# Diagonal blocks of sixteen recurrence steps computed beside the last gate tiles, and a second inverse on GpSimd there

## The chip, the cores and the metric

One core of one Trainium2 chip runs the whole kernel. The metric is the device time of one execution in microseconds (us); three timed runs of the kernel before have a median of 1893.08.

## The reference, cut to what matters

Two trunk layers over 1024 latent tokens behind 256 context tokens, 1024 channels wide. The first layer has bidirectional RWKV-7 time mixing with 12 heads of 64; the change lies in its recurrence. For each head and direction a 64 x 64 state is carried over 1280 tokens:

```python
def rwkv7_scan(r, w, k, v, kk, bb, s0, reverse):
    def step(s, inp):
        r_t, w_t, k_t, v_t, kk_t, b_t = inp
        sa = jnp.einsum('bhij,bhj->bhi', s, kk_t)
        s = s * w_t[:, :, None, :] - sa[..., None] * b_t[:, :, None, :] + v_t[..., None] * k_t[:, :, None, :]
        return s, jnp.einsum('bhij,bhj->bhi', s, r_t)
```

The output of the scan is normed, multiplied by a SiLU gate, and projected; the second layer (retention) follows and isn't touched.

## The kernel before

**Stages.** `phaseA` makes the input projection of layer one in tiles of 128 features: for each of six pairs of heads the keys, values and receptances, then the operands of the recurrence, which go to DRAM (`AR`, `BK`, `VT`). Its last four products are gate tiles (`gate_blocks`, L576), which need nothing but TensorE, a tanh on ScalarE and one product on VectorE for each of three blocks of tokens, so that their time can be shared. `phaseB` is the recurrence; `phaseCD` is everything after it.

**The recurrence in chunks.** 64 tokens make a chunk. A step handles one chunk of four (direction, pair) slots of two heads each, and 20 steps run through the 1280 tokens; three groups of pairs make NS = 60 steps in one row. Inside a chunk the sequential recurrence becomes a triangular system. For step s, `scores(s)` (L1117) multiplies the operands BK[s] and AR[s] into two PSUM tiles PSC (32 matmuls), and `masked(s)` (L1125, VectorE) writes them to the tile SC[s] with the triangle's mask. The system's 64 x 64 triangle is inverted in two halves: the two 32 x 32 diagonal blocks by substitution, row after row, and the block below them by two products (`offd1`, `offd2`) in the step before.

**The inverse of the diagonal blocks.** Eight steps make a group m, so group 0 is steps 0 to 7. `diag(s)` (L1134) stores the diagonal blocks of two steps from SC to a DRAM tile DN; `gather(s)` (L1147) loads four steps' blocks into TL, one block on each of 128 partitions; `inv(m)` (L1176) runs 31 rows, each a multiplication (L1185, tp<-zz,tl) and an addition (L1187, zz<-zz,tp), both with two SBUF operands, on VectorE for group 0 and on GpSimd for all others. Then it stores the inverse (DZ) and its turned copy (DX) on GpSimd's queue, and `bring(q)` (L1199) loads them for the four steps of q into SC and into the tile ZS (two and four loads on SP's queue). Step s can't do its `offd1(s + 1)` before bring of (s + 1) // 4.

**Order.** The order on each engine and queue is that in which the program issues; nothing is reordered. `phaseB` is a generator that the gate tiles call: once ahead of them, and then behind each of the nine pieces of a tile (four pieces of the first four k, then the rest of the three blocks in one, two and two). The first three calls load, the next eight (from behind the third piece of tile 1 to behind the first of tile 2) make scores, masks and stores of steps 0 to 7, and each call after them issues one or two rows of group 0's inverse. `rows(n)` (L1288) counts the calls (st.tick), issues a due gather or bring, and then n rows.

**Between the gates and step 0.** When the gates are done, buffers are opened on their memory; SP loads BK of five more steps into spare buffers (bky), ScalarE's queue the AR; eight steps (PR) are scored ahead, of which EA = 3 have had AR loaded during the gates; their diagonal blocks are stored from ScalarE's queue; bring(0) and bring(1) follow bky on SP's queue. Then `offd1(0)` and `offd2(0)`, and step 0.

**A step.** WT1 = scores x values (L1440, wu), its copy on ScalarE (L1441), offd1 of the next step, product with the inverse (L1454), scores of a step ahead, state (L1473 to L1479), output (L1486, L1494), offd2 and the turned operands (`tok`, L1173, from the loads br) of the next step. At the steps in CU = (2, 5, 8) one further step is scored at the end (`more`, L1391), until the scores are L = 19 steps ahead. GpSimd's rows are issued in the four slots of a step.

Of the kernel before, what the change touches and what calls it, by code (L numbers as in the profile page):

```python
# [41 lines left out]
NR = 2  # L42
CU = (2, 5, 8)
PR = 8
EZ = 1
ER = (2,1,2)
SW = 5
GB = 4
EA = 3
LL = 19  # L50
# [972 lines left out]
def phaseB(g):  # L1023
# [35 lines left out]
    def slots(pool, n0, n1, a0, a1, z):  # L1059
        for i in range(a0, a1):  # L1060
            ARR.append(pool.tile([128, 4, 128], F32, name=f"arr{i}"))
        for i in range(n0, n1, 2):
            SCP.append(pool.tile([128, 2, 4, 2, 128], F32, name=f"scr{i}"))
            SCR.extend(SCP[-1][:, j] for j in range(2))
        for i in z:
            ZS.append(pool.tile([128, 4, 4, 64], F32, name=f"zs{i}"))
            nc.gpsimd.memset(ZS[i], 0.0)

# [8 lines left out]
    TLS = [ip.tile([128, 32, 32], F32, name=f"tl{i}") for i in range(NTL)]  # L1077
    ZZT = ip.tile([128, 32, 32], F32, name="zz")
    TPT = ip.tile([128, 256], F32, name="tp")
    BR, AR, BK, VU, SC, BT, Y, PCS, DN = {}, {}, {}, {}, {}, {}, {}, {}, {}  # L1080
    st = Ctx()
# [12 lines left out]
    def load_v(k):  # L1094

        if k < NS // 2:
            VU[k] = st.rp.tile([128, 2, 4, 2, 64], F32, tag="vu", name=f"vu{k}", bufs=2)
            if k % 10 == 0:
                nc.gpsimd.memset(VU[k][0:64, 0], 0.0)
            (nc.scalar if VQ else nc.sync).dma_start(VU[k][64:128].rearrange("p c x h v -> p c x (h v)"), g.D["VT"][k // 10][:, 2 * k % 20 : 2 * k % 20 + 2])  # L1100
# [33 lines left out]
    def diag(s):  # L1134

        if s % 2 == 0:
            return
        m, c = divmod(s - 1, 8)
        if c == 0:
            DN[m] = dr.tile([2, 8 * steps(m), 32, 32], F32, tag="dn", name=f"dn{m}")  # L1140
        for b in range(2):
            bs = slice(32 * b, 32 * b + 32)
            st.q.dma_start(DN[m][b, 8 * c : 8 * c + 16].rearrange("u s t -> s u t"), pair_of(s)[bs, :, :, :, bs].rearrange("s c x h t -> s (c x h) t"))
        if c % 4 == 2:
            dgs.append((s, st.tick + TD))

    def gather(s):  # L1147
# [28 lines left out]
    def inv(m):  # L1176

        U, eng = 16 * steps(m), nc.gpsimd if m else nc.vector
        TL, ZZ, tp = TLS[m % NTL][:U], ZZT[:U], TPT[:U]
        eng.memset(ZZ, 0.0)  # L1180
# [141 lines left out]
    for s in range(E):  # L1322
# [872 lines left out]
```

## Time and profile before

| | us |
|---|---|
| median of three timed runs | 1893.08 |
| lowest, highest | 1881.7, 1895.54 |
| the profiled execution | 1888.2 |
| its span, first to last instruction | 1886.4 |

The profile is of one execution. Its page gives busy times by engine; the other views (table by stage, chain of waits, order of time of one engine, groups by line, DMA issues) are cuts of the same trace, in us from the span's start. PE is TensorE, DVE VectorE, ACT ScalarE, POOL GpSimd, SPq and ACTq the queues from which SP and ScalarE issue DMAs. L1187 is line 1187 of the kernel before. A matmul's duration overlaps the next one's, so sixteen in a row take less than their sum. "Idle before" in brackets names what released the instruction.

### The profile page before, as it was taken

What the parts mean: (1) busy time and instruction counts of PE and PEld (TensorE: products, weight loads), DVE (VectorE), ACT (ScalarE), POOL (GpSimd) and SP (SyncE); (2) the same over time, 40 slices, a digit from 0 to 9 for tenths busy, and PEclk for the clock granted to TensorE, in tenths of its full rate; (3) what the DMA queues carried; (4) which work ended last, traced back from release to release, by engine and by line L of the source; (5) the groups of instructions that cost most, each with busy time, mean ns of one, the idle gap of its engine ahead of it and who ended that gap; (6) DMA issues with size and microseconds to landing.
All of it is one profiled execution on the core that took longest, in us unless ns stands there. A gap on an engine that the chain in (4) does not pass through costs nothing.

```text
span 1886.4 us, 39626 instructions
## 1 busy us (share of the span) xinstructions
PE 1712.2 (91%) x16450; PEld 1453.3 (77%) x16450; DVE 968.8 (51%) x1524; ACT 697.1 (37%) x1538; POOL 748.3 (40%) x837
## 2 busy tenths in 40 slices
PE   6999998979888876988887878999999999999898
PEld 4777776767666776887776767889898898898786
DVE  6542589888985743444542335453443433524543
ACT  5322454635431143564564544442221311212321
POOL 4331344444442157677778311123333414414300
PEclk9999999989998987898997788999999999999999
DMA  9571265546559486677777744342111101101163
GB/s 321 173 240 59 79 180 141 158 127 187 137 155 281 142 219 166 182 205 201 206 181 164 174 145 143 134 134 83 36 46 45 45 23 57 56 23 56 51 206 100
DMA packets 326727, 257.66 MB, mean 137 GB/s; under 512 B 93756, under 2 KB 276532, under 8 KB 326292
## 3 DMA queue, kind: packets, MB, share of 16 engines
q1 hardware_dynamic: 306468, 218.16, 41.0%
q10 hardware_dynamic: 15456, 20.45, 3.7%
q0 software_dynamic: 4624, 16.52, 2.5%
q8 instruction: 130, 2.13, 0.5%
q14 instruction: 49, 0.40, 0.1%
HBM read 177.16 MB, written 77.91 MB: 135 GB/s over the span
## 4 chain that ended last, share of the span: by engine, by line
PE 44%; DMA 8%; POOL 6%; issue 5%; DVE 4%; ACT 2%; SPq 0%; ACTq 0%; POOLq 0%; DVEq 0%
PE pv L1849 6%; PE pg L1793 5%; PE pq L1793 5%; PE pk L1793 5%; PE pow_oo L1588 4%; PE pow_eo L1588 3%; POOL zz L1187 2%; POOL tp L1185 2%; PE pst L1939 2%; DMA vu<-scr_VT 2%; DMA br<-scr_BK 2%; PE psc L1123 2%; PE wu L1440 1%; PE pkc L1793 1%; PE pgb L586 1%
## 5 line engine op out<-in xcount | busy, mean ns | idle before, releaser
L531 PE MATMUL pgm<-hh,wh 128*128 128x512 f32 (+1 forms) x624 | 170.3, 382 | 0.0
L509 POOL TENSOR_TENSOR wl<-wr,wh 128x512 fp32r<-128x512 f32 x60 | 86.1, 1439 | 190.6 <-ACT wh L507 176.6
L531 PE MATMUL pgm<-hl,wh 128*128 128x512 f32 (+1 forms) x624 | 160.4, 366 | 0.4 <-POOL hl L467 0.4
L531 PE MATMUL pgm<-hh,wl 128*128 128x512 f32 (+1 forms) x624 | 160.1, 365 | 0.0
L1185 POOL TENSOR_TENSOR tp<-zz,tl 128x60 f32<-128x60 f32 (+23 forms) x217 | 110.7, 510 | 65.8 <-DMA tl<-dn 50.0
L1187 POOL TENSOR_TENSOR zz<-zz,tp 128x60 f32<-128x60 f32 (+23 forms) x217 | 118.5, 546 | 17.0
L531 PEld LDWEIGHTS pgm<-hl,wh 128*128 128x128 f32 x624 | 106.8, 195 | 21.0 <-POOL hl L467 1.5
L531 PEld LDWEIGHTS pgm<-hh,wl 128*128 128x128 f32 x624 | 106.5, 194 | 19.2
L531 PEld LDWEIGHTS pgm<-hh,wh 128*128 128x128 f32 x624 | 104.0, 197 | 20.9 <-issue 6.2
L1476 DVE TENSOR_TENSOR inc<-inc,state 128x256 f32<-128x256 f32 x54 | 23.4, 433 | 185.0 <-ACT scr L1165 73.8
L1849 PE MATMUL pv<-wv,hh 128*128 128x256 f32 x640 | 117.2, 285 | 0.0
L554 DVE SCALAR_TENSOR_TENSOR m<-pgm,dv,m 128x255 f32<-128x255 f32 (+2 forms) x108 | 105.1, 987 | 11.2 <-ACT m L544 8.4
L1849 PEld LDWEIGHTS pv<-wv,hh 128*128 128x128 f32 x640 | 99.6, 192 | 0.1
L1588 PE MATMUL pow_eo<-w_eo,yhw_eo 128*128 128x512 f32 x320 | 90.6, 405 | 0.0
L1849 PE MATMUL pv<-wv,hl 128*128 128x256 f32 x320 | 90.5, 283 | 0.0
L1129 DVE TENSOR_TENSOR scr<-psc,mask 128x512 f32<-128x512 f32 x112 | 71.7, 682 | 17.4 <-PE psc L1123 17.4
L1123 PE MATMUL psc<-arr,bkp 64*64 64x128 f32 x1728 | 71.0, 294 | 9.2 <-DVE scr L1129 3.9
L1588 PE MATMUL pow_oo<-w_oo,yhw_oo 128*128 128x512 f32 x256 | 73.3, 403 | 0.0
L1588 PEld LDWEIGHTS pow_eo<-w_eo,yhw_eo 128*128 128x128 f32 x320 | 61.3, 193 | 15.1 <-issue 0.3
L1793 PE MATMUL pg<-hh,wg 128*128 128x512 f32 x256 | 72.2, 393 | 0.0
L818 POOL TENSOR_TENSOR ar<-m,Pp 128x640 f32<-128x640 f32 (+2 forms) x30 | 36.5, 1226 | 87.0 <-ACT Pp L810 82.8
L1793 PE MATMUL pq<-hh,wq 128*128 128x512 f32 x256 | 70.1, 391 | 0.0
(347 smaller groups left out, 4227.6 us busy)
## 6 DMA issues: line engine op xcount, KB each, us to landing
aw<-ada_w SPq DMA_DIRECT2D x16, 1024.0 KB, 9.6
wr<-w_ev SPq DMA_DIRECT2D x60, 256.0 KB, 3.9
scr_AR<-ar SPq DMA_DIRECT2D x24, 640.0 KB, 3.7
scr_BK<-bk SPq DMA_DIRECT2D x24, 640.0 KB, 4.5
br<-scr_BK ACTq DMA_DIRECT2D x60, 256.0 KB, 3.8
arr<-scr_AR SPq DMA_DIRECT2D x55, 256.0 KB, 4.0
bkp<-scr_BK SPq DMA_DIRECT2D x55, 256.0 KB, 5.2
x<-xin SPq DMA_DIRECT2D x20, 512.0 KB, 4.1
```

The lines of the kernel that those rows point to most:

```text
L509: nc.gpsimd.tensor_tensor(out=wl, in0=wr, in1=wh.bitcast(F32), op=ALU.subtract)
L531: g.nc.tensor.matmul(ps[:, b, :n], lhsT=st[:, k % 4, :], rhs=mv[:, k, c0 : c0 + n], start=(k == 0 and i == 0), stop=(k == 7 and i == 2))
L554: nc.vector.scalar_tensor_tensor(out=o, in0=i, scalar=g.muc[:, q, ft : ft + 1], in1=o, op0=ALU.mult, op1=ALU.add)
L818: nc.gpsimd.tensor_tensor(out=ar[:, cs, 64:128], in0=ch(proc(self.r, d, lo, n)), in1=Pp[:, cs, 1:65], op=ALU.mult)
L1123: mm(ps[h][H[m], 128 * x : 128 * x + 128], lhsT=BK[s][H[h], x, H[m]], rhs=AR[s][H[h], x, :], start=True, stop=True, tile_position=(64 * h, ...
L1129: tt(out=out, in0=p.rearrange("p (d q t) -> p d q t", d=2, q=2), in1=K["mask2"].unsqueeze(2).broadcast_to([128, 2, 2, 128]), op=ALU.mult)
L1185: eng.tensor_tensor(out=tv, in0=ZZ[:, 0:k, s : s + 1].broadcast_to([U, k, n]), in1=TL[:, s : s + 1, s + 1 : 32].broadcast_to([U, k, n]), o ...
L1187: eng.tensor_tensor(out=zo, in0=zo, in1=tv, op=ALU.add)
L1588: self.g.nc.tensor.matmul(ps[:, 512 * b : 512 * b + 512], lhsT=st[:, k, :], rhs=mv[:, 512 * b : 512 * b + 512], start=(k == 0 and i == 0), ...
L1793: mm(ps[:, 512 * b : 512 * b + n], lhsT=st[:, k, :], rhs=mv[:, k, o : o + n], start=(k == 0 and i == 0), stop=(k == 7 and i == 2))
L1849: mm(ps[:, 256 * e : 256 * e + 256], lhsT=st[:, k, c0 : c0 + 128], rhs=mv[:, k, :], start=(k == 0 and i == 0), stop=(k == 7 and i == 2))
L1939: mm(ps[:, 128 * (i - i0) : 128 * (i - i0) + 128], lhsT=o.kz[d][:, t], rhs=o.v[:, t], start=True, stop=True)
```

## The change

During the second gate tile, behind scores(7), eight new calls `blocks(s)` (s = 8, 10, ... 22) compute only the square scores from which the diagonal blocks of steps 8 to 23 come: each loads the first 64 columns of AR and BK of two steps (two loads on SP's queue, 256 KB each in pieces of 256 B, two steps ahead of use except the first two), multiplies them (16 matmuls of 64 x 64 by 64 columns), copies the four diagonal parts on ScalarE and stores them from ScalarE's queue. No mask is applied. Groups 1 and 2 gather from there, and `diag` does nothing for these steps. Group 1's inverse is issued two rows a call from then on, beside group 0's, with temporaries of its own; group 0 must be issued to its end before the gates' memory is given up. Group 0's results are stored from SP's queue instead of GpSimd's. bring(0) is issued ahead of the loads for the scores, and bring(2) at its own time. No AR is loaded ahead for steps 8 to 10 (EA = 0), four steps are scored before step 0 instead of eight (PR), and seven steps score one more (CU). The zero fills of ZS, VU and Y2P move from GpSimd to VectorE.

```diff
-CU = (2, 5, 8)
-PR = 8
+CU = (1, 2, 3, 4, 5, 7, 9)
+PR = 4
+EB = 24
+EP = 2
-EA = 3
+EA = 0
@@ slots (and the same in load_v, and for Y2P)
-            nc.gpsimd.memset(ZS[i], 0.0)
+            nc.vector.memset(ZS[i], 0.0)
@@
-    ZZT = ip.tile([128, 32, 32], F32, name="zz")
-    TPT = ip.tile([128, 256], F32, name="tp")
+    ee = ExitStack()
+    ex = ee.enter_context(tc.tile_pool(name="exB", bufs=1, reuse_waits="tile"))
+    ZZT = [p.tile([128, 32, 32], F32, name=f"zz{i}") for i, p in enumerate((ex, ip))]
+    TPT = [p.tile([128, 256], F32, name=f"tp{i}") for i, p in enumerate((ex, ip))]
@@ diag
-        if s % 2 == 0:
+        if s % 2 == 0 or E <= s < EB:
             return
...
+    def blocks_load(s):
+
+        if s < EB:
+            DA[s], DB[s] = (ex.tile([128, 2, 4, 64], F32, tag=t, name=f"{t}{s}", bufs=2) for t in ("dka", "dkb"))
+            for o, n in ((DA, "AR"), (DB, "BK")):
+                nc.sync.dma_start(o[s], g.D[n][s // 20][:, s % 20 : s % 20 + 2, :, 0:64])
+
+    def blocks(s):
+
+        spread(s)
+        c = s % 8
+        for j in range(2):
+            for x in range(4):
+                for h in range(2):
+                    mm(PSC[h][0:64, 256 * j + 64 * x : 256 * j + 64 * x + 64], lhsT=DB[s][H[h], j, x], rhs=DA[s][H[h], j, x], start=True, stop=True, tile_position=(64 * h, 0))
+        dg = ex.tile([64, 2, 4, 2, 32], F32, tag="dg", name=f"dg{s}", bufs=2)
+        for b in range(2):
+            bs = slice(32 * b, 32 * b + 32)
+            for h in range(2):
+                nc.scalar.copy(dg[bs, :, :, h].rearrange("p c x t -> p (c x) t"), PSC[h][bs].rearrange("p (a t) -> p a t", t=64)[:, :, bs])
+            nc.scalar.dma_start(DN[s // 8][b, 8 * c : 8 * c + 16].rearrange("u s t -> s u t"), dg[bs].rearrange("s c x h t -> s (c x h) t"))
+        if c % 4 == 2:
+            dgs.append((s + 1, st.tick + TD))
+        blocks_load(s + 4)
@@ inv
-        TL, ZZ, tp = TLS[m % NTL][:U], ZZT[:U], TPT[:U]
+        TL, ZZ, tp = TLS[m % NTL][:U], ZZT[m > 0][:U], TPT[m > 0][:U]
+        out = nc.gpsimd if m else nc.sync
...
-        nc.gpsimd.dma_start(DZ, ZZ)
+        out.dma_start(DZ, ZZ)
...
-        nc.gpsimd.dma_start(DX, TL[: U // 2])
+        out.dma_start(DX, TL[: U // 2])
@@ rows
-        if back and st.tick >= back[0][1] and (back[0][0] == 0 or len(ZS) == 3 and back[0][0] != 2 and st.s >= 4 * back[0][0] - 3 - back[0][0] % 2):
+        if back and st.tick >= back[0][1] and (back[0][0] == 0 or len(ZS) == 3 and st.s >= 4 * back[0][0] - 3 - back[0][0] % 2):
@@ behind the scores of steps 0 to 7
+    def both():
+
+        n = ER[st.tick % len(ER)]
+        if ivs and ivs[0][0] == 0:
+            for _ in range(EP):
+                if len(ivs) > 1 and st.tick >= ivs[1][2]:
+                    row(1)
+            rows(n)
+        else:
+            rows(EP)
+
+    blocks_load(E)
+    blocks_load(E + 2)
+    for s in range(E, EB, 2):
+        blocks(s)
+        both()
+        yield
     while not g.a_done:
-        rows(ER[st.tick % len(ER)])
+        both()
         yield
+    while ivs and ivs[0][0] == 0:
+        row()
+    ee.close()
@@ before step 0
     st.q = nc.scalar
+    while back and back[0][0] == 0:
+        bring(*back.pop(0))
     load_v(0)
...
-    while back:
+    while back and back[0][0] < 2:
         bring(*back.pop(0))
```

## Rows read from the trace of the kernel before

**Rows 1.** The page of the profile: its span.

```profile
span 1886.4 us, 39626 instructions
```

**Rows 2.** The table by stage (core 0): a stretch in us, its length, busy us of each engine with its instructions, granted TensorE clock, busy share of the DMA engines, GB/s.

```profile
616.41:630.88 14.47, 14.12 (x73) 11.75 (x72) 13.61 (x31) 2.82 (x5) 2.58 (x2) 1.00 0.19 63
647.20:666.90 19.70, 12.48 (x293) 10.67 (x285) 10.44 (x17) 2.60 (x8) 3.95 (x7) 0.83 0.95 239
718.90:731.00 12.10, 0.25 (x6) 0.26 (x6) 0.78 (x2) 0.37 (x1) 4.79 (x10) 0.62 0.80 237
```

**Rows 3.** The chain of work that ended last, followed back from 735 us: start us, us, what.

```profile
720.58 7.17 DMA dx<-tl
727.76 2.71 DMA scr<-dx
...
730.75 0.95 PE inc L1219 x13
```

**Rows 4.** ScalarE in order of time, one line (L1441, one copy in each step; in the order shown those of steps 4, 5, 6, 7 and 15): start us, us, engine, line, operation, out<-in, shape, count, and in brackets the idle time before it and its releaser.

```profile
705.20 0.37 ACT L1441 COPY wt<-wu 128x256 f32<-128x256 f32 x1
...
713.61 0.37 ACT L1441 COPY wt<-wu 128x256 f32<-128x256 f32 x1 [2.81 <-PE wu L1440]
...
718.92 0.37 ACT L1441 COPY wt<-wu 128x256 f32<-128x256 f32 x1 [0.21 <-PE wu L1440]
...
738.30 0.37 ACT L1441 COPY wt<-wu 128x256 f32<-128x256 f32 x1 [0.22 <-PE wu L1440]
...
797.17 0.37 ACT L1441 COPY wt<-wu 128x256 f32<-128x256 f32 x1 [1.20 <-PE wu L1440]
```

**Rows 5.** TensorE in order of time, same columns: the product for step 16's off-diagonal block, in step 15.

```profile
793.31 0.98 PE L1235 MATMUL py<-zs,y2p 128*64 128x32 f32 x16 [1.94 <-DMA zs<-dz]
```

**Rows 6.** TensorE in order of time, the second of the last four gate tiles: first product behind the tile's second piece, behind its third, and the next tile's first.

```profile
606.03 0.28 PE L586 MATMUL pgb<-hh,wh 128*128 128x256 f32 x1
...
607.77 0.28 PE L586 MATMUL pgb<-hh,wh 128*128 128x256 f32 x1
...
616.41 0.28 PE L586 MATMUL pgb<-hh,wh 128*128 128x256 f32 x1
```

**Rows 7.** SP's queue (issue of step 7's diagonal blocks), and VectorE's mask of step 7 ahead of it.

```profile
607.67 0.86 SPq L1143 DMA_DIRECT2D dn<-scr  x2
...
604.28 1.29 DVE L1129 TENSOR_TENSOR scr<-psc,mask 128x512 f32<-128x512 f32 x2 [1.50 <-PE psc L1123]
```

**Rows 8.** DMA issues of the whole execution: out<-in, engine, operation, count, KB each, median us from issue to landing.

```profile
arr<-scr_AR SPq DMA_DIRECT2D x55, 256.0 KB, 4.0
bkp<-scr_BK SPq DMA_DIRECT2D x55, 256.0 KB, 5.2
```

**Rows 9.** DMA queues from 655.4 to 665.7 us, when nearly all packets were of 128 B (9567 of 9968 under 512 B): packets, MB, share of 16 engines' time.

```profile
q1 hardware_dynamic: 5576, 1.19, 54.6%
```

**Rows 10.** TensorE in order of time: sixteen matmuls with 64 columns in step 1.

```profile
680.87 0.69 PE L1486 MATMUL pyo<-scr,vu 128*64 128x64 f32 x16
```

**Rows 11.** VectorE, then GpSimd, in order of time where both read SBUF: in the last products of the operands (566 to 572), and in group 0's inverse (621.6).

```profile
566.97 0.80 DVE L820 SCALAR_TENSOR_TENSOR bk<-th,kk 128x640 f32<-128x640 f32 x1
567.99 2.07 DVE L821 TENSOR_TENSOR ar<-kk,Pp 128x640 f32<-128x640 f32 x1 [0.23 <-issue]
569.98 1.88 DVE L822 SCALAR_TENSOR_TENSOR bk<-bk,Pi 128x640 f32<-128x640 f32 x1
...
621.62 1.52 DVE L1187 TENSOR_TENSOR zz<-zz,tp 128x207 f32<-128x207 f32 x1
...
567.98 1.39 POOL L818 TENSOR_TENSOR ar<-m,Pp 128x640 f32<-128x640 f32 x1 [4.52 <-ACT Pp L810]
569.36 1.81 POOL L509 TENSOR_TENSOR wl<-wr,wh 128x512 fp32r<-128x512 f32 x1
...
621.61 1.29 POOL L509 TENSOR_TENSOR wl<-wr,wh 128x512 fp32r<-128x512 f32 x1 [10.10 <-ACT wh L507]
```

**Rows 12.** VectorE's groups of instructions by line from 620.42 to 643.0 us (rows 8 to 31 of group 0's inverse): count, busy us, mean ns, idle us before.

```profile
L1187 DVE TENSOR_TENSOR zz<-zz,tp 128x192 f32<-128x192 f32 (+15 forms) x24 | 9.9, 411 | 0.8
L1185 DVE TENSOR_TENSOR tp<-zz,tl 128x192 f32<-128x192 f32 (+15 forms) x24 | 9.7, 403 | 0.7
```

**Rows 13.** GpSimd's groups of instructions by line from 680.3 to 710.8 us (rows 1 to 24 of group 1's inverse), same columns.

```profile
L1187 POOL TENSOR_TENSOR zz<-zz,tp 128x192 f32<-128x192 f32 (+15 forms) x24 | 13.8, 576 | 1.9
L1185 POOL TENSOR_TENSOR tp<-zz,tl 128x192 f32<-128x192 f32 (+15 forms) x24 | 12.9, 538 | 30.9 <-DMA tl<-dn 29.1
```

**Rows 14.** Between the gates and step 0: VectorE's turned copy of group 0, SP's queue, and TensorE in order of time.

```profile
643.01 1.13 DVE L1192 COPY tl<-zz 64x1024 f32<-64x1024 f32 x1
...
639.08 15.13 SPq L1092 DMA_DIRECT2D bky<-scr_BK  x5
...
664.70 1.07 PE L1235 MATMUL py<-zs,y2p 128*64 128x32 f32 x16 [2.60 <-DMA zs<-dz]
666.90 1.34 PE L1440 MATMUL wu<-vu,scr 128*64 128x64 f32 x15 [1.13 <-ACT scr L1165]
```

**Rows 15.** TensorE in order of time: the transposes at the end of step 1, and the extra scores at the end of step 5.

```profile
683.03 0.63 PE L1173 MATMUL pt<-ident,br 128*128 128x128 f32 x4 [1.03 <-DMA br<-scr_BK]
...
711.21 0.43 PE L1123 MATMUL psc<-arr,bkp 64*64 64x128 f32 x4 [1.03 <-DVE scr L1129]
711.81 1.09 PE L1123 MATMUL psc<-arr,bkp 64*64 64x128 f32 x28 [0.16 <-DVE scr L1129]
```

More of the change, by code (lines that the diff above doesn't have):

```diff
@@ L1077, in phaseB @@
     TLS = [ip.tile([128, 32, 32], F32, name=f"tl{i}") for i in range(NTL)]
-    ZZT = ip.tile([128, 32, 32], F32, name="zz")
-    TPT = ip.tile([128, 256], F32, name="tp")
-    BR, AR, BK, VU, SC, BT, Y, PCS, DN = {}, {}, {}, {}, {}, {}, {}, {}, {}
+    ee = ExitStack()
+    ex = ee.enter_context(tc.tile_pool(name="exB", bufs=1, reuse_waits="tile"))
+    ZZT = [p.tile([128, 32, 32], F32, name=f"zz{i}") for i, p in enumerate((ex, ip))]
+    TPT = [p.tile([128, 256], F32, name=f"tp{i}") for i, p in enumerate((ex, ip))]
+    BR, AR, BK, VU, SC, BT, Y, PCS, DN, DA, DB = {}, {}, {}, {}, {}, {}, {}, {}, {}, {}, {}
     st = Ctx()
@@ L1098, in load_v @@
             if k % 10 == 0:
-                nc.gpsimd.memset(VU[k][0:64, 0], 0.0)
+                nc.vector.memset(VU[k][0:64, 0], 0.0)
             (nc.scalar if VQ else nc.sync).dma_start(VU[k][64:128].rearrange("p c x h v -> p c x (h v)"), g.D["VT"][k // 10][:, 2 * k % 20 : 2 * k % 20 + 2])
@@ L1134, in diag @@
     def diag(s):
-        if s % 2 == 0:
+        if s % 2 == 0 or E <= s < EB:
             return
         m, c = divmod(s - 1, 8)
-        if c == 0:
-            DN[m] = dr.tile([2, 8 * steps(m), 32, 32], F32, tag="dn", name=f"dn{m}")
+        spread(s - 1)
         for b in range(2):
@@ L1145, in diag, with spread @@
             dgs.append((s, st.tick + TD))
+    def spread(s):
+        if s % 8 == 0:
+            DN[s // 8] = dr.tile([2, 8 * steps(s // 8), 32, 32], F32, tag="dn", name=f"dn{s // 8}")
+    def blocks_load(s):
[19 more added lines that the diff above has]
+        blocks_load(s + 4)
     def gather(s):
@@ L1282, in phaseB, with row @@
     st.tick, st.wait, st.s = 0, SW, -1
-    def row():
-        if next(ivs[0][1], 0) == 0:
-            ivs.pop(0)
+    def row(i=0):
+        if next(ivs[i][1], 0) == 0:
+            ivs.pop(i)
     def rows(n):
@@ L1341, in phaseB @@
         Y2P.append(cq.tile([128, 2, 4, 64], F32, name=f"y2p{i}"))
-        nc.gpsimd.memset(Y2P[i], 0.0)
+        nc.vector.memset(Y2P[i], 0.0)
     tail.gen = tail.eg.enter_context(tc.tile_pool(name="gen", bufs=2, space=PSUM, reuse_waits="tile"))
```

## The prediction

> **What bounds the kernel now.** Start with the page and the table by stage. The profiled execution took 1888.2 us, 1.8 of them outside its 1886.4 us span [rows 1]; the sum below is made against it. The three timed runs have a median of 1893.08 and lie 13.8 us apart, so the sum may stand some 5 us under what is measured. All that changes lies between 577 and 800 us, and the table by stage [rows 2] shows that each stretch there has another limit. In the third of the last four gate tiles (616.4 to 630.9) TensorE is full, 14.12 of 14.47 us, and VectorE nearly so; between the gates and step 0 (647.2 to 666.9) TensorE is filled for 12.48 of 19.70; from 718.9 to 731.0 it stands: 0.25 us of work in 12.10.
>
> That stand is the target, and the chain of waits names its cause [rows 3]. Step 7 needs the corner blocks of steps 8 to 11. Their inverse (group 1) and its turned copy keep GpSimd until the store at 720.58, which takes 7.17 us; a load of 2.71 us follows, and TensorE goes on at 730.75. On ScalarE each step shows by one copy (L1441): 5.31 us for step 6, a plain one, 8.41 for step 5, which scores one step more, and 19.38 for step 7 [rows 4]. The stand so costs 19.38 - 5.31 = 14.1 us; the granted clock falls to 0.62 in that stretch.
>
> **Gain 1: group 1 is ready before step 7.** Its inverse is now made during the gates. By the working below it ends some 6 us after group 0's, at about 674, and is stored by 690; step 7 comes near 740. So -14.1. Nothing is next in its place there: group 2, also early, is wanted at step 15, where TensorE now waits 1.94 us for its zs [rows 5]: -1.9.
>
> **Cost 1: the second gate tile.** phaseB gets one call behind each of the nine pieces of a tile, and scores(7) stands after the first piece of tile 2, so the eight `blocks` calls stand after its other eight, the first at 606.0 [rows 6]. Its own loads are issued only there, in program order on SP's queue behind group 0's diagonal store (L1143), which waits for VectorE's mask of step 7 and went out at 607.67 [rows 7]. With six loads fewer in front I put it at 606.5 (between 605.6, the end of that mask, and 607.7). The pair of loads then goes out at 607.4 and 607.85. A load of 256 KB lands in 4.0 us (5.2 for bkp) [rows 8]; those come in rows of 2 KB, the new ones in pieces of 256 B. 128 B pieces took 54.6% of 16 engines for 10.3 us for 5576 packets, 16 ns each [rows 9], so 1024 of them keep 16 engines busy for about 1.0 us: no new bound, and I take 4.0. First wait: 607.85 + 4.0 + 0.2 - 606.0 = 6.0 us (4 to 9), with all later gate matmuls queued behind it. Each call's 16 matmuls of 64 columns cost 0.7 (16 such took 0.69, L1486 [rows 10]; bounds 0.5 and 1.0): 8 x 0.7 = 5.6. Loads for s+4 go out when blocks(s) has read its buffer: 0.65 + 4.0 + 0.15 = 4.8 us to landing, while TensorE has one piece, one call and one piece between, 4.2 at first (1.74 each, 606.03 to 607.77), then 3.5 (1.4 each, the rest to 616.41). Counting each wait as cover for the next pair leaves 0.6, 0.4, 0.9, 0.4, 0.9, 0.4 = 3.6 (0 to 9). ScalarE's four copies (0.37 each, as L1441 for as many elements a lane [rows 4]) and two issues (0.43 each, half of L1143's pair [rows 7]) per call, 2.3, fit beside this; without that cover each call would wait some 0.2. Tile 2 grows by 6.0 + 5.6 + 3.6 = 15.2 and ends at 631.6, not 616.4. On SP's queue group 0's gather now stands behind the loads for 12 and 14, and group 1's behind those for 22: it goes out near 627 and lands at 631.4.
>
> **Cost 2: two inverses on two engines.** VectorE's rows of group 0 are queued between gate products. Row 8 is behind tile 2's last one, so it moves from 620.43 to 631.6 + 0.8 (tanh) + 0.7 = 633.1. GpSimd starts group 1 at about the same moment, 631.4. What happens when both read two SBUF operands is in the trace: VectorE's L821 takes 0.80 us alone (its shape, L820) and 2.07 when GpSimd's L818 of 1.39 starts 0.01 us before it; then GpSimd's L509 takes 1.81, not 1.29, and L822 1.88. Four instructions that alone take 1.39 + 0.80 + 1.29 + 0.80 = 4.28 fill 567.98 to 571.86, 3.88: they go in turn, and only 0.1 each overlaps. In the inverse itself L1187 takes 1.52 beside an L509 [rows 11]. So the two inverses alternate. VectorE's rows 8 to 31 are 48 instructions, 9.9 + 9.7 us less 2.1 in two such collisions = 17.5 [rows 12]; GpSimd's first 24 rows are 48, 13.8 + 12.9 = 26.7 [rows 13]. In turn: 44.2 - 96 x 0.1 = 34.6 us. Gate products read PSUM and one SBUF operand and fall into GpSimd's turns. Group 0 so ends at 667.7, not 643.0; bounds: 653.6 if they never meet (the present 20.5 us), 677.3 if nothing overlaps.
>
> The Trainium skill (SBUF — State Buffer, Who interferes with whom) says more than these rows: a VectorE instruction with two SBUF inputs and a GpSimd one that reads SBUF take a shared pair of ports as an exclusive lock, and the loser blocks until the whole instruction is over. By that rule the sum would be 44.2 and the end 677.3; by the 3.88 us above, where 0.1 per instruction does overlap, it is 34.6. I take the row.
>
> **Cost 3: from there to step 0.** Now step 0 starts at 666.9 [rows 14], 24 us behind group 0's end, because bring(0) is queued on SP behind five bky loads that wait for the gates' buffers (639.08 to 654.2). After, bring(0) stands first and the bky loads behind it: copy 1.13 [rows 14] and issue 0.5, store 4.0 to landing (as a load, [rows 8]), six issues 2.6, vu 0.5 and the first bky 0.5, landing 4.0: 13.2 us; then four scores at VectorE's 1.29 a step [rows 7], 5.0; offd1, its copy, and 2.2 from py to wu: 3.8. Together 22.0: step 0 at 689.7, +22.8 (bounds 13 and 32, by the two ends of group 0). The gates' own end, about 661 to 665 with TensorE waiting for VectorE's late products in tile 4, lies under this. The zero fills moved to VectorE fall while it waits for scores; with that cover gone they cost 2 to 3 us (of the size of the 1.13 us copy for the two large ones, the others half or less). Fewer scores ahead save nothing by themselves: TensorE waited 2.60 us for zs after eight of them [rows 14].
>
> **Cost 4: four more steps with an extra score** (seven, not three). In step 5 TensorE waits 1.03 us for VectorE to free psc and then takes 711.21 to 712.83: 2.65 [rows 15]; the whole step is 8.41 - 5.31 = 3.1 longer [rows 4]. I take 2.7, by TensorE's own rows: 4 x 2.7 = 10.8. At step 1 the present wait of 1.03 for br [rows 15] should vanish under it: 9.8 (7 to 12).
>
> **Sum:** 22.8 - 14.1 - 1.9 + 9.8 = +16.6: 1888.2 + 16.6 = 1904.8, say 1905.
>
> **Rivals.** (a) The turns do not overlap at all. The 44.2 then stands whole, group 0 ends 9.6 later: 1914. The point is in the sum: above 36.9 us for the 96 instructions the kernel is slower by over 1%. For it: L1187's 1.52 is GpSimd's whole 1.29 and 0.23 more [rows 11]; against: the 3.88. (b) They hardly meet, say GpSimd starts late. Group 0 ends at 653.6; then bky at 666.8, and arr loads after the gates' end near 661, set step 0 at 675.6: 1905 - 14.1 = 1891. Against it: the gather is due 2 us before row 8. (c) Queue relief: no diagonal stores or brings for steps 8 to 23 lie in the way of steps 8 to 15. These take 58.9 us (738.30 to 797.17 [rows 4]) where eight plain steps take 42.5; less what is counted (1.9) and step 8's own extra score (2.7) that is 11.8: 1893; with (b), 1879. Against: its waits for br and vu come after step 15 as well. (d) The loads land in 5.2 us, like bkp's [rows 8], or later: 1.2 more in the first wait and in each pair, about 6: 1911. (e) Group 1 is late all the same: 14 back, 1919; 45 us of slack speak against it.
>
> **How the numbers follow.** Forecast 0.38, (a) 0.18, (b) 0.20, (c) 0.10, (b) with (c) 0.06, (d) 0.06, (e) 0.02. Leaving out the lower end of (b) with (c) and the upper ends of (a) and (d) with the timed runs' 5 us on top, the range is 1883 to 1920. One per cent is 18.9 us, about what a measurement of this kernel can tell from no change. Faster than 1869: part of (b) with (c) and gains I found no row for, 0.06. Slower than 1907: a third of the forecast, nearly all of (a) and (d), and (e): 0.36. The rest 0.58.
>
> **What would show it.** A TensorE wait of 4 to 9 us before the first block's matmuls near 606; L1185 and L1187 on VectorE near 0.9 us instead of 0.4 once GpSimd's rows run; group 0's store near 668; step 0 near 690; no wait for dx before step 8's first matmul; steps 1, 3, 4, 7 and 9 near 8 us. I am wrong if group 0 still ends before 650, or if step 0 stays below 675.

## The result and the profile after

The changed kernel takes 1901.01 us in the median of 12 runs (1889.49 to 1916.81), the kernel before 1885.84 in 12 runs beside it (1872.45 to 1895.54): a ratio of 1.0088, 95% interval 1.0061 to 1.0116. A second set, with 11 and 34 runs, gave 1.0082 (1.0050 to 1.0114). Ratios here and below leave out runs in a slower state that some executions show, and are not the quotient of the medians (1.0080 here). That is slower by 15 to 17 us and within 1%. The prediction was 1905 and +16.6 us.

The profiled execution took 1908.86 us. The page's span, and the table by stage (stretch, length, busy us of each engine with its instructions, granted clock, DMA share, GB/s) for: tile 2 from the mark below on; tiles 3 and 4; the wait behind the gates; the four scores ahead of step 0; steps 0 to 15.

```profile
span 1907.1 us, 40211 instructions
```

```profile
616.90:649.65 32.75, 24.56 (x314) 19.50 (x312) 6.31 (x19) 11.00 (x32) 1.28 (x1) 0.90 0.92 202
649.65:677.57 27.92, 27.92 (x145) 23.61 (x144) 25.61 (x48) 5.06 (x11) 20.40 (x35) 1.00 0.21 67
677.57:698.03 20.46, 0.00 (x1) 0.00 (x1) 8.77 (x14) 0.60 (x1) 17.74 (x33) 0.58 0.81 207
698.03:708.24 10.21, 8.45 (x184) 7.45 (x184) 4.97 (x8) 2.42 (x7) 7.04 (x15) 0.84 1.14 286
708.24:824.67 116.43, 101.22 (x2594) 89.07 (x2595) 62.44 (x131) 58.41 (x164) 48.45 (x86) 0.96 0.73 204
```

Where [rows 2] had TensorE standing for 12 us inside step 7, it now stands for 20.46 us between the gates and the scores. The stand has moved, and become longer. Before, TensorE was idle there for 7.2 us ([rows 2], 19.70 less 12.48) and scored on at once behind its last gate matmul (first line below, of the kernel before), from operands loaded during the gates (EA = 3). With EA = 0 the first score (second line) waits for its loads:

```profile
646.96 1.10 PE L1123 MATMUL psc<-arr,bkp 64*64 64x128 f32 x32
```

```profile
698.03 1.98 PE L1127 MATMUL psc<-arr,bky 64*64 64x128 f32 x32 [20.46 <-DMA bky<-scr_BK]
```

**A mark to measure from.** All these kernels do the same work on TensorE up to VectorE's mask of step 7 (ahead of it only one zero fill stands on VectorE instead of GpSimd, and some of SP's loads differ). In 14 profiles its end lies anywhere from 600.8 to 621.8 us: at 605.6 and 616.3 in two of the kernel before, at 616.9 and 615.3 in two of the changed one. So absolute times of two profiles can't be set side by side; the 11 us by which the changed kernel seems late there lie within that spread, whose cause isn't known. Below, times are counted from that end ("the mark").

TensorE in order of time (start us, us, engine, line, operation, out<-in, shape, count; in brackets the idle time before and its releaser), the eight block calls of tile 2:

```profile
622.53 1.77 PE L1168 MATMUL psc<-dka,dkb 64*64 64x64 f32 x32 [5.02 <-DMA dkb<-scr_BK]
...
627.07 1.15 PE L1168 MATMUL psc<-dka,dkb 64*64 64x64 f32 x32
...
630.09 1.15 PE L1168 MATMUL psc<-dka,dkb 64*64 64x64 f32 x32
...
633.55 1.15 PE L1168 MATMUL psc<-dka,dkb 64*64 64x64 f32 x32 [0.71 <-ACT dg L1173]
...
638.38 1.15 PE L1168 MATMUL psc<-dka,dkb 64*64 64x64 f32 x32 [2.09 <-DMA dkb<-scr_BK]
...
641.97 1.73 PE L1168 MATMUL psc<-dka,dkb 64*64 64x64 f32 x32
...
645.22 1.34 PE L1168 MATMUL psc<-dka,dkb 64*64 64x64 f32 x32
...
648.52 1.15 PE L1168 MATMUL psc<-dka,dkb 64*64 64x64 f32 x32 [0.38 <-DMA dkb<-scr_BK]
```

The first wait is the forecast one, 5.0 us. But a call is 32 instructions in the trace, not 16, and takes 1.15 to 1.77 us. Next GpSimd, then VectorE and GpSimd side by side, near the end of group 0:

```profile
654.76 1.30 POOL L511 TENSOR_TENSOR wl<-wr,wh 128x512 fp32r<-128x512 f32 x1 [22.45 <-ACT wh L509]
...
657.25 0.24 POOL L1218 TENSOR_TENSOR tp<-zz,tl 128x31 f32<-128x31 f32 x1
```

```profile
676.82 0.71 DVE L1218 TENSOR_TENSOR tp<-zz,tl 128x87 f32<-128x87 f32 x1
677.56 0.69 DVE L1220 TENSOR_TENSOR zz<-zz,tp 128x87 f32<-128x87 f32 x1
678.29 0.74 DVE L1218 TENSOR_TENSOR tp<-zz,tl 128x60 f32<-128x60 f32 x1
```

```profile
676.74 0.69 POOL L1220 TENSOR_TENSOR zz<-zz,tp 128x255 f32<-128x255 f32 x1
677.50 0.65 POOL L1218 TENSOR_TENSOR tp<-zz,tl 128x256 f32<-128x256 f32 x1
678.23 0.73 POOL L1220 TENSOR_TENSOR zz<-zz,tp 128x256 f32<-128x256 f32 x1
```

Pair by pair the starts lie 0.06 to 0.08 us apart: each VectorE instruction, of 87 elements or of 60, lasts as long as one of GpSimd's. GpSimd began only at 657.25, though: its queue holds a weight subtraction (L511) ahead of group 1's rows, which waits for ScalarE's cast until 654.7. SP's last gathers for group 1 went out earlier, from 645.03 on; they are the first two of these six loads, and the other four are group 2's:

```profile
645.03 9.53 SPq L1184 DMA_DIRECT2D tl<-dn  x6
```

Last ScalarE's copy of each step (L1497; steps 0, 1, 7, 8, 9 and 10 shown), the answer to [rows 4]:

```profile
708.24 0.37 ACT L1497 COPY wt<-wu 128x256 f32<-128x256 f32 x1 [0.77 <-PE wu L1496]
713.31 0.37 ACT L1497 COPY wt<-wu 128x256 f32<-128x256 f32 x1
...
759.57 0.37 ACT L1497 COPY wt<-wu 128x256 f32<-128x256 f32 x1 [0.22 <-PE wu L1496]
767.47 0.37 ACT L1497 COPY wt<-wu 128x256 f32<-128x256 f32 x1 [2.79 <-PE wu L1496]
772.78 0.37 ACT L1497 COPY wt<-wu 128x256 f32<-128x256 f32 x1 [0.21 <-PE wu L1496]
784.31 0.37 ACT L1497 COPY wt<-wu 128x256 f32<-128x256 f32 x1 [6.43 <-PE wu L1496]
```

Step 7 takes 7.90 us, not 19.38: its stand is gone. Step 8, which lost its extra score, takes 5.31.

### The profile page after: what moved, and what is told of

The parts are those of the page before. It is cut to its first block, busy times and chain, and to the rows that moved or that the text cites. A ratio compares the mean times of both kernels' runs of the same rounds, so it can differ in the third digit from the quotient of the medians.

```text
span 1907.1 us, 40211 instructions
## 1 busy us (share of the span) xinstructions
PE 1721.7 (90%) x16706; PEld 1460.4 (77%) x16706; DVE 992.4 (52%) x1532; ACT 707.8 (37%) x1570; POOL 743.4 (39%) x827
## 4 chain that ended last, share of the span: by engine, by line
PE 45%; POOL 7%; issue 5%; DMA 5%; DVE 5%; ACT 2%; SPq 0%; ACTq 0%; POOLq 0%; DVEq 0%
PE pv L1905 6%; PE pg L1849 5%; PE pq L1849 5%; PE pk L1849 5%; PE pow_oo L1644 4%; PE pow_eo L1644 3%; POOL zz L1220 2%; POOL tp L1218 2%; PE psc L1127 2%; PE pst L1995 2%; PE wu L1496 1%; DMA br<-scr_BK 1%; PE inc L1252 1%; PE pkc L1849 1%; PE wu L1510 1%
## 5 line engine op out<-in xcount | busy, mean ns | idle before, releaser
L511 POOL TENSOR_TENSOR wl<-wr,wh 128x512 fp32r<-128x512 f32 x60 | 86.8, 1451 | 212.0 <-ACT wh L509 198.0
L1296 POOL TENSOR_TENSOR rv<-rv,mhalf 128x8 f32<-128x8 f32 x15 | 24.8, 1652 | 138.6 <-DVE rv L1295 84.9
```

Of the source, the lines that this page charges most:

```text
L511: nc.gpsimd.tensor_tensor(out=wl, in0=wr, in1=wh.bitcast(F32), op=ALU.subtract)
```

## The experiments

Twelve kernels. From each one's profile, in us: the mark, step 0's copy counted from the mark, steps 0 to 15 (from step 0's copy to step 16's), and step 16's copy to step 59's.

| kernel | mark | step 0 | steps 0 to 15 | 16 to 59 | median us | ratio to before (95%) |
|---|---|---|---|---|---|---|
| before | 605.6 | 62.8 | 128.8 | 333.3 | 1885.84 | |
| before_again | 616.3 | 62.3 | 129.7 | 328.5 | 1890.93 | 0.9985 (0.9957 to 1.0013) |
| changed | 616.9 | 91.3 | 116.4 | 324.8 | 1901.01 | 1.0088 (1.0061 to 1.0116) |
| after_again | 615.3 | 91.9 | 112.0 | 323.0 | 1901.62 | 1.0082 (1.0050 to 1.0114) |
| no_turns | 600.8 | 88.4 | 117.8 | 327.7 | 1895.21 | 1.0065 (1.0032 to 1.0098) |
| early_loads | 613.8 | 85.1 | 115.8 | 326.4 | 1888.71 | 1.0042 (1.0007 to 1.0078) |
| half_blocks | 605.8 | 82.7 | 121.0 | 325.7 | 1893.19 | 1.0056 (1.0028 to 1.0084) |
| one_buffer | 614.5 | 85.5 | 114.8 | 324.2 | 1898.50 | 1.0040 (1.0010 to 1.0070) |
| bky_first | 608.0 | 88.4 | 123.1 | 330.3 | 1904.67 | 1.0051 (1.0015 to 1.0086) |
| combo | 611.1 | 75.0 | 121.1 | 330.9 | 1900.36 | 1.0043 (1.0015 to 1.0072) |
| combo_loads | 621.8 | 77.9 | 121.8 | 324.6 | 1901.41 | 1.0047 (1.0011 to 1.0083) |
| combo_half | 611.4 | 69.6 | 145.1 | 327.2 | 1910.32 | 1.0113 (1.0069 to 1.0157) |
| combo_six | 613.0 | 74.1 | 131.1 | 330.4 | 1903.25 | 1.0083 (1.0048 to 1.0117) |
| combo_last | 610.9 | 74.1 | 120.5 | 332.6 | 1887.41 | 0.9984 (0.9957 to 1.0012) |

Medians of different sets were taken on chips with other medians of the kernel before (1881.66 to 1892.88), so only the ratios compare.

**after_again, before_again: the two kernels once more, unaltered.**

> The changed kernel once more, unaltered, for a second profile. In the first pair of profiles everything up to the last score ahead of the blocks is 11.3 us later than before, though nothing there is changed, and from there to the end the changed kernel loses another 9.4 us, while the medians lie 16.6 us apart. Theory 1: the 11.3 are chance of one execution; then this profile has the first block's TensorE wait begin near 611 (not 622), and the loss from the first block to the end, against the profile before, is again larger than 9.4, near 16.6. Theory 2: the shift ahead of the stage belongs to the change (code or buffers placed otherwise): the wait begins again near 622, and the ratio near 1.009 is made half there.

> The kernel before once more, unaltered, for a second profile. In the profiles so far the end of the mask of step 7, up to which before and all changed kernels are the same, lies at 605.6 (before) and at 616.9, 615.3, 613.8, 605.8 and 600.8 (the others). From there to the last step it is 524.9 us before and 532.6 and 527.0 in two profiles of the changed kernel, while the medians lie 15 to 17 us apart. Theory 1: where that mask ends is chance; here it falls anywhere between 600 and 618, and the 524.9 before is on the long side: 518 or less here. Theory 2: the first 600 us of the changed kernel really are longer: the mask ends at 605 or below again, and the 524.9 repeats.

after_again alone spoke for its second theory: its first block's wait ended at 620.9. The other twelve profiles speak against that: kernels with the same TensorE work up to the mark reach it within a span of 21 us, and the kernel before once at 616.3. Theory 1 of before_again holds as to the mark, but its 520.5 us from there to the last step are not "518 or less".

**no_turns: group 1's rows issued only behind group 0's.**

```diff
 if ivs and ivs[0][0] == 0:
-    for _ in range(EP):
-        if len(ivs) > 1 and st.tick >= ivs[1][2]:
-            row(1)
     rows(n)
```

> GpSimd's rows of group 1 start only when VectorE has finished group 0; all else as in the changed kernel. Theory (the two inverses take turns): VectorE's rows 8 to 31 fall back from 31.0 us to the 20.5 of before, the last gate products no longer wait (they end at 683.2 in the changed kernel, 5.8 us behind TensorE's last gate matmul), and step 0 comes about 8 us earlier, held then by the gates' end and the bky loads behind it, not by group 0: the ratio to before falls from 1.009 to about 1.0045, 1894 us. Group 1 then ends near step 3, long before step 7, so no stand comes back. Rival 1: the bky loads set step 0 anyway, by buffers that come free as before: no change, 1901. Rival 2: GpSimd is late for group 2 as well and step 15 waits more: step 15 longer by several us.

A miss of the edit, not of the theory. GpSimd still began 42.6 us after the mark (40.4 in the changed kernel) and VectorE's rows 8 to 31 took 29.8 us (31.0 and 32.3). Where an instruction stands in the program binds only its own engine's queue, and nothing of group 0 is in GpSimd's.

**one_buffer: the same, and one pair of inverse buffers.** Now the data bind.

```diff
-    ZZT = [p.tile([128, 32, 32], F32, name=f"zz{i}") for i, p in enumerate((ex, ip))]
-    TPT = [p.tile([128, 256], F32, name=f"tp{i}") for i, p in enumerate((ex, ip))]
+    ZZT = ip.tile([128, 32, 32], F32, name="zz")
+    TPT = ip.tile([128, 256], F32, name="tp")
...
```

> All inverses write one pair of buffers, as in the kernel before, so that GpSimd can't start group 1 until group 0 is stored; its rows are issued behind group 0's. Merely issuing them later (the run no_turns) did not part the two: GpSimd started 42.6 us after the mask of step 7, as in the changed kernel (40.4), and VectorE's rows 8 to 31 still took 29.8. Theory: now they don't meet, rows 8 to 31 take some 21 us, the last gate product stands 1 to 2 us behind TensorE's last gate matmul, not 5.6, and step 0 comes 4 to 6 us earlier than in the changed kernel, at 86 us after that mask, not 91.5; group 1 is stored near 110, well ahead of step 7: ratio 1.005, 1892 us. Rival: the bky loads behind bring(0) take the place: the mask-to-step-0 time stays near 91.

Right. GpSimd's first group, and VectorE's row for 87 elements there:

```profile
674.91 0.95 POOL L1213 MEMSET zz<- 128x1024 f32 x1 [17.60 <-DVE gth L601]
...
676.16 0.24 POOL L1218 TENSOR_TENSOR tp<-zz,tl 128x31 f32<-128x31 f32 x1
```

```profile
669.23 0.25 DVE L1218 TENSOR_TENSOR tp<-zz,tl 128x87 f32<-128x87 f32 x1
669.51 0.25 DVE L1220 TENSOR_TENSOR zz<-zz,tp 128x87 f32<-128x87 f32 x1
```

0.25 us against 0.71. Rows 8 to 31 take 24.1 us (a little over the forecast 21), the last gate product stands 1.4 us behind TensorE's last gate matmul, not 5.6 and 6.2, and step 0 comes 6.1 us earlier than in the two profiles of the changed kernel.

**early_loads: the first two pairs of block loads behind the mask of step 5** (DB_N = 2).

```diff
         masked(s)
+        if s == 5:
+            for k in range(E, E + 2 * DB_N, 2):
+                blocks_load(k)
         diag(s)
...
-    blocks_load(E)
-    blocks_load(E + 2)
     for s in range(E, EB, 2):
```

> The first two pairs of loads for the blocks go out after the mask of step 5, ahead of its diagonal store, not behind the store of step 7; two buffers of each as in the changed kernel. Theory: the first wait of 5.0 us is gone, the later shortfalls stay (2.1 and less), tile 2 ends 5 us earlier, and with it group 0's row 8, the gates' end and step 0: -5 us, about 1896. Rival 1: step 0 is set by group 0 and its turns with GpSimd, and GpSimd's start, 657, is set by the weight casts, so that less comes through: -2 or less. Rival 2: the loads delay the diagonal stores of steps 5 and 7 and the gather of group 0, and what tile 2 gains is lost there: 0.

Right, and rather more: the first block starts 0.5 us after the mark, not 5.6, with no wait; row 8 moves from 32.9 to 27.9 and step 0 from 91.6 to 85.1. Waits of 2.9, 0.3 and 1.1 us for later pairs are left.

**half_blocks: blocks for steps 8 to 15 alone.**

```diff
-EB = 24
+EB = 16
```

> Only steps 8 to 15 have their diagonal blocks computed alone (four calls, not eight); group 2 comes from the scores again, some ten steps ahead of step 15. Theory: tile 2 is shorter by four calls of 1.2 to 1.8 us and their shortfalls, 6 to 9 us, and step 0 comes as much earlier: 1893 to 1896. Group 1's gather is on SP ahead of it no less than now, so step 7 still has no stand. Rival: group 2's diagonal stores and its gather lie again in the queues of steps 0 to 8 and its inverse on GpSimd beside the first steps: step 15 waits 1.9 or more, as before, and steps 8 to 15 give back some of the 20 us that steps 0 to 15 had gained: no change, 1901.

Both sides of it came true. Row 8 comes 8.0 us earlier and step 0 8.9; but group 2 is late, and step 15 takes 15.0 us with this wait on TensorE:

```profile
802.60 0.92 PE L1252 MATMUL inc<-scr 64*64 64x32 f32 x13 [8.21 <-DMA scr<-dx]
```

**bky_first: vu and bky loads ahead of bring(0).**

```diff
-    while back and back[0][0] == 0:
-        bring(*back.pop(0))
     load_v(0)
```

> The first vu load and the four bky loads stand ahead of bring(0) on SP's queue, as in the kernel before; all else as in the changed kernel. Theory: bring(0) holds SP from 685.5 to 689.3 there and the bky loads go out at 692.2; without it in front they go out 4 us earlier, the scores as well, bring(0) lands while they run, and step 0 comes 3 to 4 us earlier (87.5 after the mask of step 7): ratio 1.006. Rival: the loads wait for the gates' buffers just as long, bring(0) then waits behind them and lands later than the scores are done: step 0 at 91 or later.

Step 0 came 3.2 us earlier, as expected, and then took 9.9 us (5.1 and 6.4 in the changed kernel), with a TensorE wait of 2.74 for bkp.

**combo: early loads with three buffers, one pair of inverse buffers, bky first.**

> Early loads (now with three buffers of each), one pair of inverse buffers and bky loads ahead of bring(0), together. Theory: the block loads no longer make TensorE wait (10 us of waits gone), the turns are gone and bring(0) is out of the way: tile 2 ends some 8 us earlier, group 0 about 48 us after the mask of step 7, step 0 at 73 to 77 instead of 91.5; the steps as in the changed kernel: 1885 to 1888, ratio 1.000 to 1.002, at the level of the kernel before but hardly under it, since the extra scores and 8 block calls stay. Rival: the gates' own end (TensorE) and the bky loads hold step 0 at 80 or later, and the ratio stays at 1.004, that of the early loads alone.

Step 0 fell to 75.0, but the ratio is the rival's. Step 0 itself took 11.7 us. The next load in SP's queue was late, and the clock low (the table by stage, from step 0's start to the end of that wait, and from there on):

```profile
691.34 1.99 PE L1128 MATMUL psc<-arr,bkp 64*64 64x128 f32 x32 [3.91 <-DMA bkp<-scr_BK]
```

```profile
686.00:691.30 5.30, 1.44 (x34) 1.21 (x32) 0.00 (x0) 2.43 (x7) 4.67 (x9) 0.59 0.88 236
691.34:698.00 6.66, 6.66 (x112) 5.87 (x112) 2.46 (x5) 1.25 (x4) 5.91 (x10) 0.56 0.84 243
```

**combo_loads: the next three pairs of loads right behind bring(0).**

```diff
+    while back and back[0][0] == 0:
+        bring(*back.pop(0))
+    st.q = nc.sync
+    for nl in range(nl, nl + NB):
+        load_ops(nl)
+    nl += 1
+    st.q = nc.scalar
     while back and back[0][0] < 2:
         bring(*back.pop(0))
     load_group(0)
...
-        if i == NB:
-            st.q = nc.sync
-            for nl in range(nl, nl + NB):
-                load_ops(nl)
-            nl += 1
-            st.q = nc.scalar
```

> As the run combo, and the three pairs of arr and bkp loads for the scores of steps 0 to 2 stand on SP behind bring(0), not behind bring(1), the pc loads and the fourth score. In combo step 0 came 75.0 us after the mask of step 7 (91.5 in the changed kernel), but then took 11.7 us, not 5.1 to 6.4, with a TensorE wait of 3.9 for bkp, which went out at 687.3: part of what was won ahead of step 0 was handed to the next load in the queue. Theory: that wait goes, step 0 takes 7.9 or less, ratio 1.002 (4 us under combo). Rival: the loads push bring(0)'s landing or bring(1) back and step 0 comes later by as much.

The bkp wait went and step 0 still took 11.3 us, the next step 9.3: `load_group(0)`, the pc loads, now stood behind those pairs, and VectorE waited for them.

```profile
708.72 0.87 DVE L1532 TENSOR_TENSOR vu<-inc,pc 64x256 f32<-64x256 f32 x2 [12.00 <-DMA pc<-scr_PC]
```

**combo_half: with EB = 16, and group 2's rows three at a time. combo_six: with six scores ahead and five extra ones.**

```diff
-RM = {1:(3,3,3,3)}
+RM = {1:(3,3,3,3),2:(3,3,3,3)}
...
-PR = 4
+PR = 6
-CU = (1, 2, 3, 4, 5, 7, 9)
+CU = (1, 2, 3, 4, 6)
```

The second pair of edits is combo_six's alone.

> As combo_loads, with the blocks of steps 8 to 15 alone computed ahead (four calls) and group 2's rows issued three at a time as group 1's are. Theory: tile 2 shorter by four calls, 6 to 8 us, group 0 ends near 44 and step 0 comes near 68 after the mask of step 7, against 62.5 before; no stand at step 7, and step 15 waits 2 us or less for group 2 (7 us in half_blocks): step 16 near 184, before 192: ratio 0.997, the first version under the kernel before. Rival: group 2 is late again, step 15 takes 12 to 15 us, ratio 1.001.

> As combo_half, with six scores ahead of step 0 and extra scores in steps 1, 2, 3, 4 and 6 (five, not seven). Theory: an extra score costs 2.6 us in a step (7.9 against 5.3) and 1.3 ahead of step 0, where VectorE's masks set the pace, so 2 x 1.3 = 2.6 us less in all: ratio 0.9955. Rival: two more pairs of loads ahead of step 0 hold it by 2 us or more: no change against combo_half.

Step 0 came at 69.6 in combo_half, as forecast, and at 74.1 in combo_six, and both kernels then lost more than they had won: step 11 took 22.0 and 23.0 us. The norm's product for the output sits on GpSimd behind group 2's rows, which are now issued before it; TensorE's transpose waits for that.

```profile
795.75 1.11 PE L1306 MATMUL pgn<-ident,cg 128*128 128x128 f32 x4 [14.73 <-POOL cg L1299]
```

```profile
788.96 0.27 POOL L1221 TENSOR_TENSOR zz<-zz,tp 128x31 f32<-128x31 f32 x1
...
794.65 1.04 POOL L1299 TENSOR_TENSOR cg<-cg,rv 128x512 f32<-128x512 f32 x1
```

**combo_last: both of those edits put right.** RM as before, `load_group(0)` ahead of the three pairs.

> As combo_six, with group 2's rows issued again as thinly as in the kernel before, and the pc loads ahead of the three pairs of loads for steps 0 to 2. In combo_six step 11 took 23.0 us: TensorE waited 13.7 there for the norm's product on GpSimd, which stood behind group 2's last 46 rows' instructions; and VectorE waited for pc in step 0, since the pc loads stood behind those pairs. Theory: both waits were made by my own edits and go, step 11 falls to 5.3 to 8, step 1 starts 1 to 4 us earlier, and the ratio falls from 1.0083 by 14 to 16 us, to 1.000 (0.999 to 1.002): the level of the kernel before, not under it, since step 0 still comes 11 us later and steps 0 to 15 save about as much. Rival: group 2, issued thinly, is late for step 15, as in half_blocks (15.0 us), and the ratio stays at 1.004.

Right in the main: step 11 takes 9.7 us (5.3 to 8 was forecast), step 0 5.6, group 2 is not late (step 15 takes 10.5), and the ratio is 0.9984 (0.9957 to 1.0012), level with the kernel before and some 1% under the changed one, whose intervals lie wholly above it. No version here beats the kernel before by more than the measurement can tell.

## Why the prediction was right, and where its steps were not

The forecast of +16.6 us met the measured 15 to 17, but in part by luck: step 0 came 6.2 us later than forecast, and steps 0 to 15 were 8.8 us shorter. Means of the two profiles of each kernel, against the prediction:

| term | predicted | measured |
|---|---|---|
| row 8 later (tile 2), from the mark | +12.7 | +18.4 (14.6 to 32.9) |
| rows 8 to 31 (turns) | +12.0 | +9.1 (22.55 to 31.6) |
| end of group 0 to step 0 | -1.9 | +1.6 (25.5 to 27.0) |
| step 0 | +22.8 | +29.0 (62.6 to 91.6) |
| steps 0 to 15 | -6.2 | -15.0 (129.3 to 114.2) |
| sum | +16.6 | +14.0 |

Step 16 to step 59, whose program the change leaves alone, came out 7.0 us shorter in the two profiles of the changed kernel, and what lies behind the last step 1.5 longer. The other kernels, the same there, spread from 324 to 333, so I take the 7.0 for chance; without it the profiles give +15.5, with it +8.5. That reading is argued, not shown: two profiles of each can't size a few us.

**Cost 1, tile 2: mis-sized.** The step that failed is "each call's 16 matmuls of 64 columns cost 0.7": the count came from the loops and the price from a row of 16 instructions [rows 10], but each matmul of the program leaves two records: a call is 32, as a score is, and the row of 16 is eight matmuls. The eight calls together take 10.6, not 5.6: 1.15 each at a granted clock of 1.00, and up to 1.77 at the lower level. The first wait (5.0 for 6.0) and the later ones (3.2 in all, 4.4 in after_again, for 3.6) were right. Tile 2 as a whole grew by 21.9 us (first profile of each), where 15.2 were put: the lower clock behind the waits was no term of the sum. From 624.22 to 627.07 the table by stage has it at 0.65, and nine gate matmuls take 2.85 us that take 1.94 further on. The run early_loads removes the first wait and half_blocks half of the calls; they move row 8 by 5.0 and 8.0.

**Cost 2, turns: right in kind, too dear.** They cost 7.5 us (31.6 against one_buffer's 24.1), and were put at 12.0. The 12.0 counted on GpSimd from 631.4, 25.8 us after that profile's mark; it started at 40.4, since the gathers went out 6.7 us later (28.1 behind the mark for 21.4) and its own weight subtraction stood in front until 39.2, so that VectorE's rows 8 to 15 ran nearly alone. That is part of rival (b), which would have needed them hardly to meet. Where they do meet, the price per instruction was wrong too: the prediction added both engines' times, less 0.1 us each. Near the end of group 0 the rows show GpSimd untouched. Its starts for 255 and 256 elements lie 0.73 to 0.80 us apart beside VectorE (676.74, 677.50, 678.23, and 679.03), and 0.72 to 0.82 alone, in one_buffer:

```profile
693.04 0.68 POOL L1220 TENSOR_TENSOR zz<-zz,tp 128x255 f32<-128x255 f32 x1
693.80 0.65 POOL L1218 TENSOR_TENSOR tp<-zz,tl 128x256 f32<-128x256 f32 x1
694.52 0.73 POOL L1220 TENSOR_TENSOR zz<-zz,tp 128x256 f32<-128x256 f32 x1
695.34 0.64 POOL L1218 TENSOR_TENSOR tp<-zz,tl 128x255 f32<-128x255 f32 x1
```

There VectorE alone pays: it gets through one instruction for each of GpSimd's, of 87 elements or of 60. A stretch of n of VectorE's instructions beside GpSimd's longer ones so costs n of GpSimd's periods, and not the sum of both. GpSimd isn't spared everywhere: its first 17 rows, L511 left out, took 21.8 us, against 20.7 for group 2's with no rows of VectorE beside them, and the addition that it began inside VectorE's copy (L1225, from 680.76) took 1.24 us, not 0.68:

```profile
681.29 1.24 POOL L1220 TENSOR_TENSOR zz<-zz,tp 128x252 f32<-128x252 f32 x1
```

The Trainium skill (SBUF — State Buffer, Who interferes with whom) has the engine that issues first hold the shared ports for its whole instruction, and the other blocked. VectorE's 0.25 that became 0.71 agrees with that; that GpSimd then waits out VectorE's instruction in its turn does not show here: by that a pair would take 0.69 + 0.25 = 0.94 us, and it takes 0.73.

**Cost 3: the queue behind group 0.** 22.0 were put from group 0's end to step 0's first matmul, and 26.4 and 25.4 are measured (27.0 in the mean to its copy, as in the table). The prediction had the gates end under this. They did not: VectorE's last gate product is queued behind the slowed rows and ends 5.6 us after TensorE's last gate matmul, 2.5 us after group 0; the gates' stores follow it, and the first loads go into the gates' buffers (in combo, SP's waits ahead of bky name those stores, scr_G<-gth, for 4.5 us). SP issues the vu load at 690.88 and bky at 692.18:

```profile
680.75 0.35 SPq L1224 DMA_DIRECT2D dz<-zz  x1
682.13 0.48 SPq L1227 DMA_DIRECT2D dx<-tl  x1
685.53 0.86 SPq L1237 DMA_DIRECT2D scr<-dx  x2
686.48 2.83 SPq L1242 DMA_DIRECT2D zs<-dz  x4
690.88 0.48 SPq L1104 DMA_DIRECT2D vu<-scr_VT  x1
692.18 2.27 SPq L1096 DMA_DIRECT2D bky<-scr_BK  x4
```

The chain of waits to the first score runs through the first arr load, on ScalarE's queue behind the gates' stores, and the first bky load, which goes out as that one lands (what makes it wait for that, the trace doesn't tell):

```profile
687.34 4.82 DMA arr<-scr_AR
692.18 5.80 DMA bky<-scr_BK
```

The sum had no term for arr there, and 4.0 for bky. So the path that held step 0 went through the gates' end and these loads, more than through group 0's store and bring(0). one_buffer bears this out: there group 0 ends 5.6 us ahead of the last gate product, and from group 0's end to step 0's copy it takes 28.0 us, no less than here. bky_first, with bring(0) out of the way of bky, gave back 3.2. What EA = 0 costs by itself, and PR = 4, no run tests apart.

**Gain 1 and cost 4: right.** Step 7 went from 19.4 to 8.0 with an extra score of 2.6 in it, 14.0 for the forecast 14.1. A step with an extra score takes 7.89, a plain one 5.31: 2.6 for the forecast 2.7. But the four more cost less on balance, since they fell on waits of before: steps 1, 3, 4, 8 and 9 together grew by 2.8 us, and with step 7's 2.6 that is 5.4, where 9.8 were put. Nor did step 15 gain its 1.9 as such: its zs wait is gone and one for bkp of 2.2 and 1.7 us stands there.

**What was not in the sum: step 0's clock.** Step 0 took 9.7 us before and 5.7 after, -3.9. Some 1.2 of that is a wait for bkp in it (1.39 and 1.11 us in the two profiles before) that is gone. The rest goes with the clock. In the kernel before TensorE's gaps ahead of step 0, the 2.60 us wait among them [rows 14], leave it at the lower level; in the changed kernel four scores fill 698.03 to 704, with the clock at 0.50 in the first half and 0.95 in the second. The table by stage for step 0 before, and for step 0 after:

```profile
668.38:678.12 9.74, 8.35 (x138) 7.40 (x140) 2.46 (x5) 3.52 (x11) 0.00 (x0) 0.54 0.99 272
```

```profile
708.24:713.31 5.07, 4.89 (x138) 4.41 (x139) 2.27 (x5) 3.53 (x10) 4.44 (x9) 1.00 0.68 234
```

The same 138 instructions take 8.35 us of TensorE at 0.54 and 4.89 at 1.00. In combo, where step 0 came 16.6 us earlier, it ran at 0.56 to 0.59 again.

**What was to show it.** The wait of 4 to 9 us came (5.0), VectorE's rows went to 0.71 us (0.9 was given), group 0's store went out 64.6 us after the mark (62.4 by 668), and steps 1, 3, 4 and 7 take 7.9 to 8.1; step 9 does not (11.5 and 9.8, with waits of 3.2 and 1.9 for vu); step 0's first matmul was due near 690, 84.4 after the mark, and began at 707.10, 90.2 after it.

**Rivals.** (c), queue relief in steps 8 to 15, was put at 11.8 us: they take 55.0 against 57.8 (means of two), 2.8 less; it did not come. (d), loads of 5.2 us or more: the block loads landed in 3.3 to 5.0 (medians of dka and dkb in two profiles), and the waits were hardly longer than forecast. (e) did not come: no changed kernel waits for group 1 in step 7 (what TensorE waits for there, up to 5.9 us in combo_six, are loads of vu and br). (a) is refuted by GpSimd's rhythm above: a pair takes 0.73 us, less than the sum of both.

## What to carry to other kernels

A stand that was removed by moving its work forward was paid for at the new place: 14 us were won in step 7, and 29 spent ahead of step 0, of which combo had 16.6 back and then lost 7 of them again in steps 0 to 15. Each time the next entry of an in-order queue was late instead (bkp, then pc, then the norm's product on GpSimd), so ask of each edit what stands behind it in the queue, not only what it frees. To keep two engines apart, bind them by data or by a queue that both must pass; the place in the program alone does not.

## What the runs showed of the hardware

Where GpSimd and VectorE, with two SBUF operands each, ran back to back and GpSimd's instructions were the longer ones, they did not share the loss: GpSimd kept its 0.73 us per instruction, and VectorE's 0.25 became 0.70 (674 to 680 us of the changed kernel's profile). It is no general rule: beside VectorE's copy GpSimd took 1.24 us instead of 0.68, and in [rows 11] its L509 took 1.81 instead of 1.29. Two executions of one program reached the same instruction at 605.6 and 616.3 us, and fourteen of kernels with the same TensorE work ahead of it at 600.8 to 621.8; only times counted from a mark could be compared. Behind the 5.02 us wait in tile 2, up to which the granted clock was 1.00, the first block call ran at 0.58 and took 1.77 us, not the 1.15 of a call at 1.00: that wait cost more than its own length. In combo 6.66 us of matmuls at 0.56 followed a wait of 3.9 us, but the clock had begun to fall (0.82) in the 1.4 us ahead of that wait.
